# Attention scores as two matmuls of 128 rows instead of one of 128 and one of 64

## Chip, cores and metric

The kernel runs on one core of one Trainium2 chip. The metric is the device time of one execution in microseconds (us), lower is better; the median of the timed runs stands for a kernel.

## The reference

Two layers of a decoder trunk on 512 tokens of width 1024, in float32. Each layer projects the modulated and normalised tokens once (`h @ w_in`), feeds three mixers with the columns (a state-space mixer, a stick-breaking attention with 8 heads of 64, and a sparse attention with 8 query heads of 64 on 2 key heads, whose keys an indexer with 8 heads of 64 chooses), merges the three with gates, and ends in a squared-ReLU MLP. Three places multiply queries with keys over 64 channels; they are what the change touches:

```python
# stick-breaking attention, per block of 128 queries
z = jnp.einsum("bthd,bshd->bhts", q[:, s0:e0], k[:, :e0]) * scale
# sparse attention: the indexer's scores ...
logits = jnp.einsum("bthd,bsd->bths", q_idx[:, s0:e0], k_idx[:, :e0]) * (IDX_DIM ** -0.5)
# ... and the attention's own
s = jnp.einsum("btgrd,btkgd->btgrk", qb, k_sel) * scale
```

## The kernel before

All products of float32 numbers are made in parts: a number is kept as H, rounded to the matmul's fp32r format, and L, the rest. A projection (`mm3`, L198 to L201) is three matmuls into one PSUM bank: H with H, L with H and H with L. `tile_trunk` makes the whole program. Projections are jobs of 256 columns, cut into pieces of four blocks of 128 rows of the contraction; a piece's weights are loaded on SP's queue (`emit_split`, L448), rounded on ACT (L460) and their rest is taken on DVE (L461), two pieces ahead. Between the projections run streams of other work, one generator each: `scores` (the indexer), `topk`, `sbatt`, `dsa`, `ssd`. `run` (L504) is a planner: it adds up estimated costs of PE and DVE and emits the next step of a stream or the next two blocks of a projection. The order of emission is the priority of the scheduler that orders each engine's instructions; the list `ORDER` (L39) gives the order of the jobs.

The score product is `qk` (L212 to L216). A block of two heads comes out of a projection with the upper head on partitions 0 to 63 and the lower one on 64 to 127. `stack` (L203) makes of it one tile for each head, over all 128 partitions, with three copies on SP's queue (L209): for queries the head's H part above its L part, for keys its H part twice. Then one matmul over 128 rows (L215) gives (H + L of q) with H of k, and a second over the head's own 64 rows (L216) gives H of q with L of k, which is read from the tile that the evacuation left. Query tiles are the stationary operand (128 columns), keys the moving one (128 to 512 columns, by the causal block).

`qk` is called 24 times a layer by `scores` (L798; its key is doubled by ACT copies at L693 and L694), 32 times by `sbatt` (L858) and 32 times by `dsa` (L976). Keys come from the four jobs `qk0` to `qk3` (`evac_hl`, L823) and from `dkv` (`evac_dkv`, L957). All these tiles come from the pool `pa` of 26 tiles of 128 x 512 (L159). `fin` of `sbatt` (L901) ends a block of two heads and gives back its tiles; it is `sb.0` to `sb.3` in the planner's names. The projections have three accumulator banks, `acc` (L177), and a job takes two; the scores have two banks, `qk` (L180).

Of the kernel before, what the change touches and what calls it, by code (L numbers as in the profile page):

```python
# [17 lines left out]
P = 128  # L18
# [39 lines left out]
class Piece:  # L58
    """A part of a job's weights along the contraction."""

# [9 lines left out]
class Unit:  # L70
    """The products of a piece with some of the tokens."""

# [11 lines left out]
class Job:  # L84
    """A projection of one or two blocks of 128 columns, cut along its contraction."""

# [20 lines left out]
def paired(fin, a, b):  # L107
    """The units of two jobs, both with the first half of the tokens before the second."""
    a.fin = b.fin = fin
    a.left = b.left = 2  # L110
    ps = a.pieces() + b.pieces()
    for p in ps:
        p.keep = True
    return [Unit(p, c) for c in HALVES for p in ps]


class Stream:
    """Work beside the projections. A step yields its cost in us on PE and DVE and is told when its results are
    expected; it can also yield the time before which the next step is not to be emitted, or what it needs finished."""

# [30 lines left out]
def tile_trunk(ctx: ExitStack, tc: tile.TileContext, io, out, depth=DEPTH):  # L151
# [50 lines left out]

    def stack(H, L, same):  # L203
        """For the upper and the lower head of a block, one tile each over all partitions: the parts of the head,
        or its first part twice; the first part stays on the partitions that it was on."""
        B = pa.tile([P, T], F32R, name="paS", tag="pa")
        S = H if same else L
        for o, i in ((B[64:128, :], H[64:128, :]), (B[0:64, :], S[64:128, :]), (H[64:128, :], S[0:64, :])):
            sync.dma_start(o.bitcast(F32), i.bitcast(F32))  # L209
        return H, B, L  # L210

    def qk(ps, q, k, hh, cq, ck):  # L212
        """Three products of parts of 64 rows, two of them in one pass"""
        r = slice(hh * 64, hh * 64 + 64)
        pe.matmul(ps, q[hh][:, cq], k[hh][:, ck], start=True, stop=False)  # L215
        pe.matmul(ps, q[hh][r, cq], k[2][r, ck], start=False, stop=True)  # L216

    # ---- vectors of the layers, as columns over the partitions
    rows = [pa.tile([P, P], F32, name="rows", tag="pa") for _ in range(3)]
# [3 lines left out]
    sync.dma_start(crow, io["c"].rearrange("o (r c) -> (o r) c", c=P))  # L223
    # ---- constants
    slab = const.tile([P, 3216], F32, name="slab")
# [20 lines left out]

    # ---- silu(c) as columns
    cth = fixed(NK)
# [8 lines left out]
    tc.keep_in_program_order(act.preload_act_table_set("natural_log_exp_and_others"))  # L257
    # a column that adds up what the first of 32 partitions hold, for each half of the partitions
    pick = fixed(2)
# [38 lines left out]
    def ada_first(i):  # L298
        """What two of the blocks of 128 channels of layer 0 need first, shift and scale: two parts of 256 columns, each
        in two halves along the contraction, on PE beside each other in its columns."""  # L300
        wv = io["ada_w"][0].rearrange("(k p) c -> p k c", p=P)
# [49 lines left out]
    def rstd_cols(s_, r_, q_):  # L351
        """From sums of squares, one token on a partition"""
        dve.tensor_scalar(s_, s_, 1.0 / D, EPS, op0=ALU.mult, op1=ALU.add)
        act.activation(r_, s_, AF.Ln)
        act.activation(r_, r_, AF.Exp, scale=-0.5)
        dve.tensor_mul(q_, r_, r_)
        dve.tensor_mul(q_, q_, s_)
        dve.tensor_scalar(q_, q_, -0.5, 1.5, op0=ALU.mult, op1=ALU.add)
        dve.tensor_mul(r_, r_, q_)

    # ---- x, feature-major, and the norm of its tokens
    xin = [None] * 4
# [17 lines left out]

    # ---- norms
    class SumSq:
# [4 lines left out]
        def tile(self, key, c):  # L387
            """A temporary, the same one for both halves of the tokens"""
            if c == ALL:
                return tmp()  # L390
            if key not in self.kept:
                self.kept[key] = tmp()
            return self.kept.pop(key) if c == HALVES[1] else self.kept[key]
# [27 lines left out]
    class Modulated:  # L421
        """x normalised, scaled and shifted per channel, in two parts"""

# [74 lines left out]
    def later(f, lat=1.8):  # L498
        """Have f emitted when what has been emitted so far is expected to be done."""
        j = clock["job"]  # L500
        j.open += 1
        waiting.append((max(clock["pe"], clock["dve"]) + lat, j, f))

    def run(items, ahead=2, step=2):  # L504
        """Emit the units of the jobs in order and the steps of the streams between them. The order of emission
        is the scheduler's priority, so a step is emitted when its operands are expected to be there."""
        live = []
# [112 lines left out]
    def begin(l):  # L620
        """What the layer needs from its start on."""
        ly = {"A1": fixed(8), "A2": fixed(8),
              "h": Modulated(), "rs": rstd_tile()}
        return ly
# [8 lines left out]
    def layer(l, lys):  # L633
# [12 lines left out]

        # ---- small vectors of the SSD mixer
        dtb = fixed(1)[:16, :]
# [25 lines left out]

        # ---- index key, index weights, dt
        iwT = fixed(24).rearrange("p (a b) -> p a b", a=3)
# [9 lines left out]
        def evac_misc(i, ps):  # L686
# [7 lines left out]
            act.copy(iL[64:128, :], iL[0:64, :])  # L694
            st["ik"] = (iH, iH, iL)

# [7 lines left out]
        def dtprep():  # L704
            # D per channel
            dsr = fixed(8)[:16, :]
# [8 lines left out]
            dve.tensor_scalar(na, na, -1.0, None, op0=ALU.mult)  # L715
            # dt = softplus(raw + bias)
            s8 = st["dt"]
# [13 lines left out]
            yield 0, 3.4, 3.0  # L731
            # dt * a and its running sum in each chunk
            dve.tensor_scalar(u, g, na, None, op0=ALU.mult)
# [16 lines left out]
            yield 0.4, 0.4  # L750
            # the sum of each chunk on all partitions
            dg = fixed(64)[:16, :].rearrange("p (a b) -> p a b", a=16)
# [16 lines left out]
        def evac_iq(j):  # L769
            def f(i, ps):  # L770
                H, L = hl()
                rope(ps, H, L)
                iq[2 * j + i] = stack(H, L, False)
            return f

        # ---- the indexer: scores and the top 128 of each row
        sc = [None] + [tf.tile([P, T], F32, name="sc", tag="acb", bufs=6)[:, :(tb + 1) * P] for tb in range(1, 4)]
# [40 lines left out]

        # ---- stick-breaking attention
        sbt = {}  # L820
        ysb = yp.tile([P, 4, T], F32R, name="ysbH", tag="yH"), yp.tile([P, 4, T], F32R, name="ysbL", tag="yL")

        def evac_hl(key):  # L823
            def f(i, ps):
                H, L = hl()
                split(ps, H, L)
                sbt[key[i]] = stack(H, L, i == 1)
            return f
# [15 lines left out]
        def sbatt():  # L844
            """Per head: weights = sigmoid(z) times the product of (1 - sigmoid(z)) over the later keys."""
            qunits = [[3], [2, 0], [1]]
# [45 lines left out]
            def d_step(j, po, two):  # L892
                """both heads of a block beside each other in the columns of PE"""
                vb = sbt["v", j].rearrange("p (t d) -> p t d", t=4)
# [50 lines left out]

        # ---- sparse attention
        ydsa = [None, None]
        dq = {}

        def evac_dq(j):  # L950
            def f(i, ps):
                H, L = hl()
                rope(ps, H, L, 0.125)
                dq[2 * j + i] = stack(H, L, False)
            return f

        def evac_dkv(i, ps):  # L957
            if i == 0:
                H, L = hl()
                rope(ps, H, L)  # L960
                dq["k"] = stack(H, L, True)
            else:
                evac_v([None, "dv"])(1, ps)

        def dsa():
# [31 lines left out]
            def d_step(tb, g, po, a, s):  # L997
                """the upper and the lower heads of the blocks beside each other in the columns of PE"""
                av = a.rearrange("p (a b t) -> p b a t", a=2, b=2)
# [52 lines left out]

        # ---- SSD mixer
        sd = {}
# [55 lines left out]
        def ssd():  # L1110
            sst["ss"] = SumSq()

            def tok(qd, cp, sc_):
                """x token-major times a factor per token and head, for two chunks, in two parts"""
                xs = [sd["xs", 2 * qd], sd["xs", 2 * qd + 1]]
# [16 lines left out]
            def prep(qd, q):  # L1132
                """chunk states and what they give: y = D x + the part from earlier chunks"""
                g = qd // 2
# [48 lines left out]
            def e_step(qd, n):  # L1183
                """decay between the tokens of a chunk times C B"""
                h = 4 * qd + n
# [14 lines left out]
            def d_step(q, m, two):  # L1200
                """two heads beside each other in the columns of PE"""
                pd = qk_bank()
# [54 lines left out]

        # ---- merge
        mg = {}
# [175 lines left out]

        # ---- MLP
        w_up = io["w_up"][l].rearrange("(k p) c -> p k c", p=P)
# [88 lines left out]

    # ---- the start: what the first half of the contraction needs, then the second
    lys = {}
# [74 lines left out]
```

## Time and profile before

| | us |
|---|---|
| timed runs | 2067.71, 2056.53, 2066.98 |
| median | 2066.98 |
| profiled execution: span from the first to the last instruction | 2054.7 |
| PE busy | 2029.1 (99%), 9940 matmuls |
| DVE busy | 1282.9 (62%) |
| ACT busy | 879.6 (43%) |
| mean granted TensorE clock | 0.987 |

The profile is one execution; it lists its span, and not what the timed run has around it. PE is the engine of the matmuls, PEld its weight loads, DVE the vector engine, ACT the scalar engine, SP the engine whose queue issues most transfers. A matmul's duration runs from its start to the end of its last result, so consecutive ones overlap; how long a stream takes is read from their starts. Shapes are given as rows x columns of the stationary operand and then the output.

### The profile page before, as it was taken

Reading aid. Unit: us, or ns where it says so; the run is one execution under the profiler, and the core shown is the slowest. Engines: PE = TensorE matmul, PEld = TensorE weight load, DVE = VectorE, ACT = ScalarE, POOL = GpSimd, SP = SyncE. Lnnn points to the kernel's source line nnn. Section 1 sums busy time; section 2 is a strip of 40 time slices with the busy share of each in tenths; the row PEclk is TensorE's granted clock in tenths of the full one; section 3 lists DMA queues with packets and bytes.
Section 4 is the critical chain, followed back from the end, with each engine's and each line's share of the span. In section 5 each row is a group of like instructions: output and inputs, shape, how many; then the busy total and the mean of one; then the engine's idle time right before and its main releaser. Section 6 shows DMA issues by size and latency. Waiting matters only on the chain.

```text
span 2054.7 us, 26669 instructions
## 1 busy us (share of the span) xinstructions
PE 2029.1 (99%) x9940; PEld 1622.4 (79%) x9940; DVE 1282.9 (62%) x2368; ACT 879.6 (43%) x1562; POOL 86.1 (4%) x135
## 2 busy tenths in 40 slices
PE   8999999999999999999999999999999999999998
PEld 5667777588888988888896777767888898888887
DVE  4779767887846887333476985578576473333334
ACT  4444543743434533242444535267235254233343
POOL 0100110000000000000000101101000000000000
PEclk9879999999999999999999999999999999999999
DMA  9724254354344686332334423414333332323221
GB/s 293 221 83 138 69 140 122 108 163 133 115 133 144 225 294 233 93 103 92 112 98 115 113 77 75 113 52 129 108 103 108 123 113 83 99 94 105 93 93 42
DMA packets 247222, 254.36 MB, mean 124 GB/s; under 512 B 33348, under 2 KB 207732, under 8 KB 247092
## 3 DMA queue, kind: packets, MB, share of 16 engines
q1 hardware_dynamic: 246512, 252.52, 40.2%
q8 instruction: 78, 1.28, 0.2%
q14 instruction: 52, 0.43, 0.1%
q10 hardware_dynamic: 356, 0.14, 0.0%
q0 software_dynamic: 224, 0.00, 0.0%
HBM read 232.81 MB, written 6.42 MB: 116 GB/s over the span
## 4 chain that ended last, share of the span: by engine, by line
PE 95%; DMA 2%; DVE 1%; ACT 0%; issue 0%; POOL 0%; SPq 0%; ACTq 0%; POOLq 0%; DVEq 0%
PE acc L199 26%; PE acc L200 26%; PE acc L201 26%; PE qk L216 3%; PE qk L215 2%; PE tr L992 1%; PE po L1001 1%; PE tr L885 1%; PE po L898 1%; PE qk L1207 1%; PE po L201 1%; PE po L200 1%; PE po L199 1%; DMA araw<-in_ada_w_dram 1%; PE qk L199 1%; PE qk L200 1%
## 5 line engine op out<-in xcount | busy, mean ns | idle before, releaser
L199 PE MATMUL acc<-aH,wH 128*128 128x512 f32 x1544 | 619.0, 401 | 1.0 <-DVE tmp L665 0.6
L201 PE MATMUL acc<-aH,wL 128*128 128x512 f32 x1544 | 610.3, 396 | 0.9 <-DVE wL L461 0.9
L200 PE MATMUL acc<-aL,wH 128*128 128x512 f32 x1544 | 609.7, 395 | 0.0
L460 ACT CAST wH<-raw 128x1024 fp32r<-128x1024 f32 (+2 forms) x290 | 295.2, 1026 | 306.4 <-PE acc L200 269.0
L461 DVE TENSOR_TENSOR wL<-raw,wH 128x1024 fp32r<-128x1024 f32 (+2 forms) x290 | 342.9, 1198 | 24.5 <-PE acc L201 11.4
L199 PEld LDWEIGHTS acc<-aH,wH 128*128 128x128 f32 x1544 | 292.0, 189 | 69.8 <-issue 10.5
L201 PEld LDWEIGHTS acc<-aH,wL 128*128 128x128 f32 x1544 | 291.9, 189 | 64.8 <-issue 2.4
L200 PEld LDWEIGHTS acc<-aL,wH 128*128 128x128 f32 x1544 | 292.3, 189 | 60.7 <-issue 3.8
L199 PE MATMUL acc<-uH,wH 128*128 128x512 f32 x448 | 174.9, 390 | 0.0
L201 PE MATMUL acc<-uH,wL 128*128 128x512 f32 x448 | 174.6, 390 | 0.0
L200 PE MATMUL acc<-uL,wH 128*128 128x512 f32 x448 | 174.3, 389 | 0.0
L193 DVE TENSOR_TENSOR uL<-tmp,uH 128x512 fp32r<-128x512 f32 x64 | 43.9, 691 | 188.4 <-ACT uH L192 188.3
L1494 ACT ACTIVATE tmp<-acc 128x512 f32<-128x512 f32 x60 | 35.3, 593 | 220.0 <-PE acc L201 220.0
L1507 DVE SCALAR_TENSOR_TENSOR x<-acc,slab,x 128x512 f32<-128x512 f32 (+1 forms) x64 | 43.8, 716 | 129.2 <-PE acc L201 129.2
L334 DVE SCALAR_TENSOR_TENSOR aacc<-araw,slab,aacc 128x512 f32<-128x512 f32 x140 | 104.6, 753 | 7.0 <-DMA araw<-in_ada_w_dram 5.4
L201 PEld LDWEIGHTS acc<-uH,wL 128*128 128x128 f32 x448 | 84.1, 188 | 17.4
L200 PEld LDWEIGHTS acc<-uL,wH 128*128 128x128 f32 x448 | 84.1, 188 | 17.4
L199 PEld LDWEIGHTS acc<-uH,wH 128*128 128x128 f32 x448 | 84.1, 188 | 17.2
L873 DVE TENSOR_TENSOR_SCAN tmp<-tmp 128x512 f32<-128x512 f32 (+1 forms) x64 | 52.5, 824 | 31.2 <-ACT tmp L866 31.1
L666 POOL TENSOR_TENSOR tmp<-tmp,slab 128x512 f32<-128x512 f32 (+1 forms) x20 | 31.6, 1578 | 720.2 <-DVE tmp L665 689.9
L1315 DVE SCALAR_TENSOR_TENSOR tmp<-tg,acc 128x512 f32<-128x512 f32 x16 | 11.0, 685 | 68.2 <-PE acc L201 68.2
L813 DVE MAX8 m<-sc 128x8 f32<-128x256 f32 (+2 forms) x96 | 52.8, 554 | 1.0
(307 smaller groups left out, 3071.5 us busy)
## 6 DMA issues: line engine op xcount, KB each, us to landing
araw<-in_ada_w_dram SPq DMA_DIRECT2D x192, 256.0 KB, 5.3
raw<-in_w_in_dram SPq DMA_DIRECT2D x96, 512.0 KB, 3.8
raw<-in_w_up_dram SPq DMA_DIRECT2D x64, 512.0 KB, 4.6
raw<-in_w_down_dram SPq DMA_DIRECT2D x64, 512.0 KB, 3.7
raw<-in_w_in_dram SPq DMA_DIRECT2D x56, 256.0 KB, 4.4
acb<-acd SPq DMA_DIRECT2D x32, 256.0 KB, 4.5
raw<-in_w_br_ssd_dram SPq DMA_DIRECT2D x16, 512.0 KB, 5.1
raw<-in_w_out_dram SPq DMA_DIRECT2D x16, 512.0 KB, 4.2
```

Source lines behind the costliest of these rows:

```text
L193: dve.tensor_sub(L, src, H)
L199: pe.matmul(ps, a[0], b[0], start=start, stop=False)
L200: pe.matmul(ps, a[0], b[1], start=False, stop=False)
L201: pe.matmul(ps, a[1], b[0], start=False, stop=stop)
L215: pe.matmul(ps, q[hh][:, cq], k[hh][:, ck], start=True, stop=False)
L216: pe.matmul(ps, q[hh][r, cq], k[2][r, ck], start=False, stop=True)
L334: dve.scalar_tensor_tensor(a, raw, cs[:, k:k + 1], a, op0=ALU.mult, op1=ALU.add)
L460: act.copy(H[:, :w], src)
L461: dve.tensor_sub(L[:, :w], src, H[:, :w])
L813: dve.max(out=m8, in_=sc[tb])
L873: dve.tensor_tensor_scan(out=nv, data0=nv, data1=nv, initial=1.0, op0=ALU.mult, op1=ALU.bypass)
L1507: dve.scalar_tensor_tensor(xt[m][:, c], ps[:, c], mod[l][:, M_G2 + m:M_G2 + m + 1], xt[m][:, c], op0=ALU.mult, op1=ALU.add)
```

## The change

`qk` becomes two matmuls of 128 rows with the same stationary tile: the head's H above L with the key's H part twice, and again with the key's L part twice. `stack` keeps its form for queries only, and a new helper, `twice`, makes two pairs of tiles of a key block: its H part twice for each head, and its L part twice for each head. It adds a tile and three copies for a key block. The product of L with L, which was left out before, is now included. The index key already had both parts on both halves, and its tuple is written anew.

```diff
-    def stack(H, L, same):
+    def stack(H, L):
         B = pa.tile([P, T], F32R, name="paS", tag="pa")
-        S = H if same else L
-        for o, i in ((B[64:128, :], H[64:128, :]), (B[0:64, :], S[64:128, :]), (H[64:128, :], S[0:64, :])):
+        for o, i in ((B[64:128, :], H[64:128, :]), (B[0:64, :], L[64:128, :]), (H[64:128, :], L[0:64, :])):
             sync.dma_start(o.bitcast(F32), i.bitcast(F32))
-        return H, B, L
+        return H, B
+
+    def twice(H, L):
+        out_ = []
+        for X in (H, L):
+            B = pa.tile([P, T], F32R, name="paS", tag="pa")
+            for o, i in ((B[64:128, :], X[64:128, :]), (B[0:64, :], X[64:128, :]), (X[64:128, :], X[0:64, :])):
+                sync.dma_start(o.bitcast(F32), i.bitcast(F32))
+            out_.append((X, B))
+        return out_
 
     def qk(ps, q, k, hh, cq, ck):
-        r = slice(hh * 64, hh * 64 + 64)
-        pe.matmul(ps, q[hh][:, cq], k[hh][:, ck], start=True, stop=False)
-        pe.matmul(ps, q[hh][r, cq], k[2][r, ck], start=False, stop=True)
+        for n in range(2):
+            pe.matmul(ps, q[hh][:, cq], k[n][hh][:, ck], start=n == 0, stop=n == 1)
...
-            st["ik"] = (iH, iH, iL)
+            st["ik"] = ((iH, iH), (iL, iL))
...
-                iq[2 * j + i] = stack(H, L, False)
+                iq[2 * j + i] = stack(H, L)
...
-                sbt[key[i]] = stack(H, L, i == 1)
+                sbt[key[i]] = (stack, twice)[i](H, L)
...
-                dq[2 * j + i] = stack(H, L, False)
+                dq[2 * j + i] = stack(H, L)
...
-                dq["k"] = stack(H, L, True)
+                dq["k"] = twice(H, L)
```

## Rows read from the trace of the kernel before

**Rows 1.** The page's chain that ended last, by engine and by line.

```profile
PE 95%; DMA 2%; DVE 1%; ACT 0%; issue 0%; POOL 0%; SPq 0%; ACTq 0%; POOLq 0%; DVEq 0%
PE acc L199 26%; PE acc L200 26%; PE acc L201 26%; PE qk L216 3%; PE qk L215 2%; PE tr L992 1%; PE po L1001 1%; PE tr L885 1%; PE po L898 1%; PE qk L1207 1%; PE po L201 1%; PE po L200 1%; PE po L199 1%; DMA araw<-in_ada_w_dram 1%; PE qk L199 1%; PE qk L200 1%
```

**Rows 2.** The matmuls of L216: durations in ns, first and last start, shapes.

```profile
L216 PE MATMUL qk<-paL,paH x88: 322/435/792, 75.0 to 1387.9; 64*128 64x256 f32 x24, 64*128 64x384 f32 x24, 64*128 64x512 f32 x24, 64*128 64x128 f32 x16
L216 PE MATMUL qk<-paL,paS x88: 322/435/792, 76.3 to 1393.6; 64*128 64x256 f32 x24, 64*128 64x384 f32 x24, 64*128 64x512 f32 x24, 64*128 64x128 f32 x16
```

**Rows 3.** Timeline of PE, one pair of 512 columns: start us, duration us, what.

```profile
142.31 0.39 PE L201 MATMUL acc<-aH,wL 128*128 128x512 f32 x1
142.53 0.39 PE L215 MATMUL qk<-paS 128*128 128x512 f32 x1
142.85 0.49 PE L216 MATMUL qk<-paL,paS 64*128 64x512 f32 x1
143.27 0.50 PE L199 MATMUL acc<-aH,wH 128*128 128x512 f32 x1
143.61 0.40 PE L200 MATMUL acc<-aL,wH 128*128 128x512 f32 x1
```

**Rows 4.** Timeline of the weight loads of the same pair; idle before in brackets.

```profile
142.31 0.19 PEld L215 LDWEIGHTS qk<-paS 128*128 128x128 f32 x1
142.85 0.18 PEld L216 LDWEIGHTS qk<-paL,paS 64*128 64x128 f32 x1 [0.35 <-issue]
```

**Rows 5.** Timeline of PE, a pair of 256 columns, second layer.

```profile
1092.72 0.28 PE L215 MATMUL qk<-paH 128*128 128x256 f32 x1
...
1093.57 0.40 PE L200 MATMUL acc<-aL,wH 128*128 128x512 f32 x1
```

**Rows 6.** Timeline of PE, projections of 256 columns in a row.

```profile
674.49 0.28 PE L199 MATMUL qk<-aH,paH 128*128 128x256 f32 x1
674.61 0.28 PE L200 MATMUL qk<-aL,paH 128*128 128x256 f32 x1
```

**Rows 7.** L216 alone in one stretch: stretch, us, PE and PEld busy, PEclk, DMA.

```profile
88.40:125.90 37.50, 12.98 (x18) 5.13 (x18) 0.50 0.34 94
```

**Rows 8.** Timeline of PE inside that stretch.

```profile
114.48 0.63 PE L200 MATMUL acc<-aL,wH 128*128 128x512 f32 x1
114.91 0.63 PE L215 MATMUL qk<-paH 128*128 128x512 f32 x1
...
117.64 0.79 PE L201 MATMUL acc<-aH,wL 128*128 128x512 f32 x1
```

**Rows 9.** Six stretches: us, PE, PEld, DVE, ACT, POOL busy, PEclk, DMA share, GB/s.

```profile
73.00:124.00 51.00, 49.43 (x122) 27.83 (x122) 31.64 (x67) 21.13 (x39) 0.88 (x3) 0.65 0.48 130
137.00:300.00 163.00, 163.00 (x748) 121.78 (x747) 136.35 (x285) 79.09 (x137) 22.08 (x38) 1.00 0.44 123
324.00:420.00 96.00, 95.21 (x459) 64.79 (x458) 71.14 (x192) 57.97 (x138) 3.69 (x6) 0.98 0.34 103
1092.00:1124.00 32.00, 32.00 (x117) 19.18 (x117) 25.61 (x55) 16.70 (x33) 3.26 (x4) 1.00 0.40 109
1124.00:1290.00 166.00, 166.00 (x758) 123.17 (x759) 128.86 (x286) 83.39 (x146) 19.01 (x40) 1.00 0.32 87
1320.00:1400.00 80.00, 78.86 (x364) 52.68 (x363) 51.84 (x155) 45.90 (x112) 3.28 (x5) 0.96 0.26 77
```

**Rows 10.** The copies of L209 on SP's queue: ns, first and last; landing us.

```profile
L209 SPq DMA_DIRECT2D paS<-paH x44: 461/467/587, 57.8 to 1315.5; - x44
...
DMA to landing us min/median/max: 2.2/2.3/4.4
```

**Rows 11.** Timeline of ACT: ends of `sb.0` and `sb.1` (L901), `qk2`'s evacuation (L192).

```profile
180.64 0.60 ACT L901 ACTIVATE ysbH<-po 128x512 fp32r<-128x512 f32 x1 [3.01 <-PE po L898]
...
189.16 0.59 ACT L192 CAST paH<-acc 128x512 fp32r<-128x512 f32 x1 [3.93 <-PE acc L201]
...
234.11 0.58 ACT L901 ACTIVATE ysbH<-po 128x512 fp32r<-128x512 f32 x1
```

## The prediction, made before the changed kernel was run

> **What bounds the kernel now.** I read the chain of waits first. It gives TensorE (PE) 95% of the span, and the two lines of the score product (L215 and L216) 5% of it, so about 103 us of 2054.7 [rows 1]. The reader should see that nothing else holds the end for long: a microsecond taken from PE is a microsecond of the kernel unless another engine becomes late. The second view is the list of one line's instructions, for the counts: L216 runs 88 times on the one key tile and 88 times on the other, so there are 176 score products, 48 each of 512, 384 and 256 columns and 32 of 128 [rows 2]. The third is the timeline of PE around one product, read by starts and not by durations, since the passes overlap. In the stream of projections a 512-column pass starts 0.22 to 0.23 us after the one before it. The 64-row pass starts 0.32 us after the 128-row one, the next projection 0.42 us after that, and the one behind it 0.34 us later [rows 3]. The weight loads say why: the load of the 128-row pass begins while the pass before it streams, but that of the 64-row pass begins only with its own pass, after 0.35 us of idle [rows 4]. So changing from 128 rows to 64 and back is paid at both edges.
>
> **The change, part by part.**
>
> *The second pass grows to 128 rows.* With 512 columns, from the start of L215 to the second start behind the pair is 143.61 - 142.53 = 1.08 us [rows 3]. Three equal 128-row passes would take 3 x 0.227 = 0.68, so the pair costs 0.40 us too much. With 256 columns the same stretch is 1093.57 - 1092.72 = 0.85 us [rows 5]; two passes of 256 columns at the stream's 0.12 us and a projection at 0.227 make 0.47 [rows 3, 6], so 0.38 too much. The excess hardly depends on the width: it is an edge, not a streaming time. The operation that replaces it, two 128-row passes into one bank with the same stationary tile, is not in the trace. The nearest rows are the three passes of a projection, which also accumulate in one bank, and I take their step. Bounds: 0 saved, if the second load of the same tile can't go ahead; 0.40 saved by the stream. I take 0.38, nearest to the stream, and 176 x 0.38 = 67 us.
>
> *The low clock.* In the score stage of the first layer the granted clock is 0.50 (1.2 GHz) for 37.5 us, with 18 of the pairs in it [rows 7]. There two pairs of 512 columns take 117.64 - 114.91 = 2.73 us, where four projection steps of 0.43 would take 1.72 [rows 8]: 0.50 too much per pair, so 18 x (0.50 - 0.38) = 2 us more. Ahead of the fall PE ran score pairs between small transposes; it rose behind the pairs, in unbroken projections. The same stage of the second layer keeps 1.00 [rows 9]. If the change leaves no broken stretch, the clock could stay up or recover at once: about 30 projection passes at 0.23 instead of 0.43 give 6 us, 36 score passes at half of their low-clock time, (8 x 0.86 + 8 x 0.64 + 2 x 0.43) / 2 by their widths, another 6. Bounds 0 and 12 us. I take 6, since the rows show a stage at either level and the pairs are only one of the things in it.
>
> PE alone: 67 + 2 + 6 = 75 us.
>
> *What is late next.* The six stages that hold the pairs show VectorE (DVE) close behind PE [rows 9]. Second layer's scores: DVE is busy 25.6 of 32.0 us, so of 24 x 0.38 = 9 us at most 6.4 can come off unless its work moves; I take 6. First layer's scores: 6 x 0.38 + 18 x 0.50 + 6 = 17 us would leave 51 - 17 = 34 against DVE's 31.6; I take 13. The two stick-breaking and two sparse stages hold 32 pairs each, 12 us each: 163 - 12 = 151 against 136.4, 166 - 12 = 154 against 128.9, 96 - 12 = 84 against 71.1, 80 - 12 = 68 against 51.8. DVE fits, at 76% to 90%, but with chains through ScalarE (ACT) and back; I take 80% of 4 x 12 = 39 us. Sum: 13 + 6 + 39 = 58 us.
>
> *The lower key part held twice.* Each of ten key blocks (four `qk` jobs and `dkv`, two layers) gets one more tile and three more copies of 128 KB on SP's queue. A copy issues in 0.47 us and lands after 2.3 us [rows 10]. The third copy overwrites what the second reads, so it can hold the queue until that has landed: 3 x 0.47 + 2.3 = 3.7 us for a block, and behind it wait the weight loads of the projections and the `ada` loads. I cost this at nothing, because weights are issued two pieces ahead and a piece of four rows of blocks keeps PE for 24 x 0.227 = 5.4 us; if that cover is gone, it costs up to 10 x 3.7 = 37 us. The other end is 0: nothing of it can gain. No first use is near: `qk2`'s evacuation starts at 189.2 us and its heads come after the end of `sb.1` at 234.1 [rows 11]. The index key was already held twice in both parts, so it adds nothing.
>
> *Queries and labels.* Only the tuple shrinks: the lower query tile was read by nothing but its copies. No cost, no gain.
>
> The sum is against the profiled execution: 2054.7 us of span, to 1996.7. What lies around the span isn't in the page; the timed runs are 1.8 to 13.0 us above it, their median 12.3, which I keep: 1996.7 + 12.3 = 2009 us.
>
> **The rivals.**
>
> *A: the edges go and most of it reaches the end.* 2009 us; from 2067 - 82 = 1985 (all of PE's 75 us, and 6 more from the clock) to 2030. For: [rows 1, 3, 4]. Chance 0.70.
>
> *B: DVE becomes the bound.* PE's edges go, but the stages stop at DVE's and ACT's pace: 8 us in the first scores, 3 in the second, half of 48 in the others, 35 us together: 2032 us, up to 2045. For: DVE's 78% to 84% in three stages [rows 9]. Against: it is idle there while PE is not, so it waits for PE. Chance 0.15.
>
> *C: the second load can't go ahead.* Every 128-row pass of the pair would then start like the one behind the change of rows, 0.34 us after the last [rows 3], and so would the projection behind it: 3 x 0.34 = 1.02 against 1.08 us, 0.06 x 176 = 11 us, 2056 us. The Trainium skill (TensorE: Matmul & The Clock Gate, Part 3, The mechanism) speaks for this: it says that a weight load overlaps a running matmul only when its row group differs, and both passes now use all rows. The trace disagrees: loads over all 128 rows go ahead in every step of the stream, and it is the load with other rows that waits [rows 4]. Chance 0.03.
>
> *D: the copies eat the gain.* SP's 37 us come onto the path and DVE takes what B says: 35 - 37, about 2069 us, no change. For: L209's copies sit in the same queue as the weights. Against: the cover of 5.4 us per piece. Chance 0.06.
>
> *E: slower, by the pool of 26 tiles.* A `qk` block now holds six tiles instead of five. If `qk2` is evacuated before the heads of `qk0` are done, the pool would hold 3 x 6 for `qk0`, `qk1` and `qk3`, 2 for `v0`, and 3 + 4 for `qk2`, so 27 of 26, where now it is 15 + 2 + 6 = 23. The evacuation would wait for `sb.0`, holding two of the three accumulator banks, and projections stop. Now `sb.0` ends 8.5 us before [rows 11]. The price of a wait is at most the distance between the ends of two such steps, 234.1 - 180.6 = 53 us, in each layer: 2 x 53 - 58 = 48 us slower, 2115 us. It decides from (58 + 10) / 2 = 34 us per layer. Chance 0.06.
>
> **How the numbers follow.** The likeliest is A, 2009 us. A and B hold 0.85; the range goes from A's end, 1985, to B's, 2045, and leaves out C, D, E and what little lies below. About 0.5% (10 us) is what a measurement of this kernel can tell from no change. Faster: A, B and C, 0.88 (C by a hair). Same: D, 0.06. Slower: E, 0.06.
>
> **What would show it.** Right: in the timeline both score passes start 0.22 us after one another at 512 columns, the load of the second has no idle ahead of it, and the projection behind starts at the stream's step; the two score lines fall from 5% of the chain to about 3%; the first score stage spends less than 37 us at 0.50, and the six stages shorten by some 14, 6 and four times 10 us. B would show as waits of PE's loads for DVE in these stages, C as an idle ahead of the second load, D as ACT's weight casts waiting for w_in, E as ACT's evacuation of `qk2` behind the end of `sb.0` with PE idle. The prediction is wrong if the schedule of the whole program comes out in another order, since a planner places every step and I assume that it leaves them where they are.

## The result, and the profile after

| | before | after |
|---|---|---|
| median of 4 runs, us | 2061.76 | 1994.89 |
| lowest and highest, us | 2056.06, 2067.71 | 1993.62, 1997.39 |
| profiled execution: span, us | 2054.7 | 1992.6 |
| PE busy, us | 2029.1 | 1955.4 |
| mean granted clock | 0.987 | 0.996 |

The ratio of after to before is 0.969, with a 95% interval of 0.966 to 0.972: 3.1% faster. The forecast was 2009 us, with a range of 1985 to 2045 and 0.88 for faster. The time is 14 us under the forecast.

The chain of waits of after, from its page (shares of the span, by engine and then by line; L225 is the line of the score matmuls now):

```profile
PE 88%; DVE 7%; DMA 2%; issue 1%; ACT 1%; POOL 0%; SPq 0%; ACTq 0%; POOLq 0%; DVEq 0%
PE acc L199 25%; PE acc L201 25%; PE acc L200 25%; PE qk L225 2%; DVE wL L470 1%; PE po L1010 1%; PE tr L1001 1%; DVE sc L823 1%; DVE m L822 1%; DVE tmp L882 1%; PE po L907 1%; PE qk L1216 1%; PE tr L894 1%; DMA araw<-in_ada_w_dram 1%; PE po L201 1%
```

Against [rows 1], the score lines fall from 3% and 2% to 2% together, and DVE goes from 1% to 7%, with the top-k lines L822 and L823 in it, which the chain of before did not show. So the edges left PE's path, and DVE took a part of it.

The edges themselves are seen in PE's timeline of after, around a pair of 512 columns (start us, duration us, what), and in the timeline of the weight loads of two such pairs in a row:

```profile
106.70 0.39 PE L201 MATMUL acc<-aH,wL 128*128 128x512 f32 x1
106.93 0.39 PE L225 MATMUL qk<-paH 128*128 128x512 f32 x1
107.15 0.39 PE L225 MATMUL qk<-paL,paH 128*128 128x512 f32 x1
107.38 0.39 PE L199 MATMUL acc<-aH,wH 128*128 128x512 f32 x1
107.61 0.39 PE L200 MATMUL acc<-aL,wH 128*128 128x512 f32 x1
```

```profile
100.05 0.19 PEld L225 LDWEIGHTS qk<-paH 128*128 128x128 f32 x1
100.28 0.19 PEld L225 LDWEIGHTS qk<-paL,paH 128*128 128x128 f32 x1
100.51 0.19 PEld L225 LDWEIGHTS qk<-paH,paS 128*128 128x128 f32 x1
100.74 0.19 PEld L225 LDWEIGHTS qk<-paL,paS 128*128 128x128 f32 x1
100.97 0.19 PEld L201 LDWEIGHTS acc<-aH,wL 128*128 128x128 f32 x1
```

From the first pass of the pair to the second start behind it is 107.61 - 106.93 = 0.68 us, where before had 1.08 [rows 3]. Each pass starts 0.22 to 0.23 us after the one before it, and no load has idle ahead of it, where the 64-row load had 0.35 us [rows 4]. With 256 columns the second pass starts 0.11 us after the first.

What took part of the gain back is in PE's waits of after, the two longest that before did not have (engine and line, what it waited for: us in total, times, longest), and in PE's timeline:

```profile
PE acc L199 <- DVE paL L193: 5.0, 1, 5.0
PE acc L199 <- DVE ysbL L911: 3.4, 1, 3.4
```

```profile
161.82 0.76 PE L225 MATMUL qk<-paS 128*128 128x384 f32 x4
162.42 0.62 PE L894 MATMUL tr<-slab,tmp 128*128 128x128 f32 x4
168.02 0.80 PE L199 MATMUL acc<-aH,wH 128*128 128x512 f32 x1 [4.98 <-DVE paL L193]
168.61 0.63 PE L200 MATMUL acc<-aL,wH 128*128 128x512 f32 x1
169.04 0.63 PE L201 MATMUL acc<-aH,wL 128*128 128x512 f32 x1
```

The next job's projection needs an accumulator bank, and the bank comes free when DVE has taken the rest of a key block out of it (L193). DVE's timeline shows what stands ahead of that instruction:

```profile
163.14 0.55 DVE L823 MATCH_REPLACE8 sc<-m,sc 128x384 f32<-128x384 f32 x1
163.60 0.14 DVE L885 TENSOR_SCALAR tmp<-tmp 128x1 f32<-128x1 f32 x1
163.72 0.56 DVE L822 MAX8 m<-sc 128x8 f32<-128x384 f32 x1
...
166.22 1.15 DVE L822 MAX8 m<-sc 128x8 f32<-128x384 f32 x2
167.29 0.67 DVE L193 TENSOR_TENSOR paL<-acc,paH 128x512 fp32r<-128x512 f32 x1
```

From 163.07 to 167.29 DVE runs top-k almost back to back while PE has nothing. PE then comes back at the lower clock: projection passes step by 0.43 us from 168.61 to 172.45. The wait in the second layer, at 1133.85, looks the same: L911 starts at 1133.12 behind top-k, and from 1135.42 to 1138.41 the passes step by 0.43 us.

Last, the stretches of [rows 9] in after. The first is the same stretch; the second and third hold the work of [rows 9]'s two stick-breaking stages, 25 to 27 and 45 to 50 us earlier (columns as there):

```profile
73.00:124.00 51.00, 49.23 (x235) 39.50 (x233) 48.43 (x110) 33.22 (x61) 4.73 (x8) 1.00 0.78 208
112.10:272.60 160.50, 155.42 (x748) 122.46 (x747) 138.70 (x290) 77.59 (x138) 22.43 (x38) 0.98 0.51 136
1079.30:1239.80 160.50, 156.84 (x760) 123.32 (x759) 132.15 (x290) 82.46 (x147) 19.87 (x40) 0.99 0.39 100
```

The first stretch went from clock 0.65 to 1.00 and holds 235 matmuls instead of 122. In the other two PE, which was busy all the time before, is idle for 5.1 and 3.7 us.

Where the time went is read by counting the projections' matmuls (L199 to L201) and comparing the start of the same one in both traces:

```
work of before, us                      gain of after by its end   in the stage   predicted
first scores (73 to 137)                24.9                       24.9           13
first stick-breaking (to 300)           27.4                        2.5           10
first sparse (to 420)                   38.7                       11.3           10
up to the second scores (to 1092)       38.2                       -0.5            0
second scores (to 1124)                 44.8                        6.6            6
second stick-breaking (to 1290)         50.4                        5.6           10
second sparse (to 1400)                 63.0                       12.6           10
to the end                              62.9                       -0.1            0
```

### The profile page after: what moved, and what is told of

The parts are those of the page before. It is cut to its first block, busy times and chain, and to the rows that moved or that the text cites. A ratio compares the mean times of both kernels' runs of the same rounds, so it can differ in the third digit from the quotient of the medians.

```text
span 1992.6 us, 26735 instructions
## 1 busy us (share of the span) xinstructions
PE 1955.4 (98%) x9940; PEld 1609.0 (81%) x9940; DVE 1279.8 (64%) x2368; ACT 872.1 (44%) x1562; POOL 87.9 (4%) x135
## 4 chain that ended last, share of the span: by engine, by line
PE 88%; DVE 7%; DMA 2%; issue 1%; ACT 1%; POOL 0%; SPq 0%; ACTq 0%; POOLq 0%; DVEq 0%
PE acc L199 25%; PE acc L201 25%; PE acc L200 25%; PE qk L225 2%; DVE wL L470 1%; PE po L1010 1%; PE tr L1001 1%; DVE sc L823 1%; DVE m L822 1%; DVE tmp L882 1%; PE po L907 1%; PE qk L1216 1%; PE tr L894 1%; DMA araw<-in_ada_w_dram 1%; PE po L201 1%
## 5 line engine op out<-in xcount | busy, mean ns | idle before, releaser
L199 PE MATMUL acc<-aH,wH 128*128 128x512 f32 x1544 | 612.3, 397 | 9.4 <-DVE paL L193 5.0
L201 PE MATMUL acc<-aH,wL 128*128 128x512 f32 x1544 | 606.7, 393 | 0.9 <-DVE wL L470 0.8
L200 PE MATMUL acc<-aL,wH 128*128 128x512 f32 x1544 | 605.7, 392 | 0.0
L470 DVE TENSOR_TENSOR wL<-raw,wH 128x1024 fp32r<-128x1024 f32 (+2 forms) x290 | 343.0, 1198 | 18.8 <-ACT wH L469 7.9
L199 PEld LDWEIGHTS acc<-aH,wH 128*128 128x128 f32 x1544 | 290.8, 188 | 72.0 <-DVE paL L193 5.7
L201 PEld LDWEIGHTS acc<-aH,wL 128*128 128x128 f32 x1544 | 290.8, 188 | 62.6 <-DVE wL L470 2.2
L200 PEld LDWEIGHTS acc<-aL,wH 128*128 128x128 f32 x1544 | 291.2, 189 | 57.7 <-issue 0.7
L199 PE MATMUL acc<-uH,wH 128*128 128x512 f32 x448 | 174.9, 390 | 0.0
L201 PE MATMUL acc<-uH,wL 128*128 128x512 f32 x448 | 174.6, 390 | 0.0
L200 PE MATMUL acc<-uL,wH 128*128 128x512 f32 x448 | 174.3, 389 | 0.0
L193 DVE TENSOR_TENSOR uL<-tmp,uH 128x512 fp32r<-128x512 f32 x64 | 43.9, 692 | 187.8 <-ACT uH L192 187.8
L201 PEld LDWEIGHTS acc<-uH,wL 128*128 128x128 f32 x448 | 84.1, 188 | 17.6
L200 PEld LDWEIGHTS acc<-uL,wH 128*128 128x128 f32 x448 | 84.1, 188 | 17.3
L199 PEld LDWEIGHTS acc<-uH,wH 128*128 128x128 f32 x448 | 84.1, 188 | 17.1
L822 DVE MAX8 m<-sc 128x8 f32<-128x256 f32 (+2 forms) x96 | 52.6, 551 | 1.2 <-POOL sc L800 0.2
```

Of the source, the lines that this page charges most:

```text
L193: dve.tensor_sub(L, src, H)
L199: pe.matmul(ps, a[0], b[0], start=start, stop=False)
L200: pe.matmul(ps, a[0], b[1], start=False, stop=False)
L201: pe.matmul(ps, a[1], b[0], start=False, stop=stop)
L470: dve.tensor_sub(L[:, :w], src, H[:, :w])
L822: dve.max(out=m8, in_=sc[tb])
```

## The experiments

All ratios are to the kernel before on the same chip, with 95% intervals. The tables of gains go by the same count of projections.

**Do the copies and the new order matter without the 128-row passes?** The changed kernel with the second pass back on 64 rows:

```diff
-        for n in range(2):
-            pe.matmul(ps, q[hh][:, cq], k[n][hh][:, ck], start=n == 0, stop=n == 1)
+        r = slice(hh * 64, hh * 64 + 64)
+        pe.matmul(ps, q[hh][:, cq], k[0][hh][:, ck], start=True, stop=False)
+        pe.matmul(ps, q[hh][r, cq], k[1][hh][r, ck], start=False, stop=True)
```

> The changed kernel with its second score pass back on 64 rows; the doubled lower key part and its copies stay. Theory of the edges (the gain is the change of rows and the clock that came with it): the time is that of the kernel before, 2062 us within 10, and the first score stage runs at 0.50 again. Rival (the gain came from another order of the program, or from tiles and copies): it stays below 2030 us. Copies not hidden: above 2070 us.

2044.49 us, ratio 0.994 [0.992, 0.997]. That is neither of the two values: with the same passes as before and 30 copies more, the kernel is no slower and a little faster. The whole difference is gained in the first score stage (15.7 us between 75 and 137 us of the profiled executions, and 1.5 us either way at most afterwards), and the stage's line says why:

```profile
73.00:124.00 51.00, 49.43 (x189) 32.00 (x188) 40.87 (x87) 28.97 (x52) 2.62 (x6) 1.00 0.64 169
```

The clock is 1.00, where the same 64-row pairs had 0.65 in [rows 9]. What differs on PE is only the order: the copies moved some of the scheduler's choices, and in the traces 106 of PE's 9940 matmuls stand in other places than in before, all of them between 84 and 136 us. So the fall of the clock does not follow from the pairs alone. This is one profiled execution: six of the ten runs lie at 2041 to 2045 us like it, with a mean clock of 0.995 to 0.998, and four at 2050 to 2053 us with 0.990 to 0.992; where those four lost their time is not known. From here to after, the 128-row passes give 49.6 us, 0.28 for each of 176 pairs; in the first score stage, at 1.00 in both, 24.8 - 15.7 = 9.1 us, 0.38 for each of 24.

**Do the copies cost anything?** The changed kernel without the copies of the lower key part; the second pass multiplies 128 rows of the unstacked tile, which holds the L parts of both heads. The query's H still meets its own head's L, but the query's L meets the L of the other head, a small product that does not belong there:

```diff
-        for X in (H, L):
-            ...
-            out_.append((X, B))
-        return out_
+        B = pa.tile([P, T], F32R, name="paS", tag="pa")
+        for o, i in ((B[64:128, :], H[64:128, :]), (B[0:64, :], H[64:128, :]), (H[64:128, :], H[0:64, :])):
+            sync.dma_start(o.bitcast(F32), i.bitcast(F32))
+        return [(H, B), (L, L)]
```

> The changed kernel without the copies of the lower key part (the second pass of 128 rows reads the part as it was left, so the scores of the key blocks are not the right ones): the price of the tile and the three copies. Copies hidden: 1995 us within 6. Copies on the path: up to 37 us less, 1958 us, and least of all places in which a wait ahead of the score passes names a DMA.

1987.47 us, ratio 0.966 [0.963, 0.968]; 7.4 us under after. In the traces DVE keeps the order of before in all its 2368 places, where after has 286 changed, and the two waits of 5.0 and 3.4 us are gone. The first stretch is at 1.00 here too, with before's order on PE (one score pass stands three places later) and without 64-row passes:

```profile
73.00:124.00 51.00, 49.32 (x238) 40.26 (x237) 49.26 (x115) 33.58 (x63) 4.36 (x8) 1.00 0.75 208
```

**Is it the transfers or the order that they force?** The same copies on POOL's queue instead of SP's, and beside it the changed kernel once more:

```diff
-                sync.dma_start(o.bitcast(F32), i.bitcast(F32))
+                (sync if X is H else pool).dma_start(o.bitcast(F32), i.bitcast(F32))
```

> The changed kernel with the copies of the lower key part issued on GpSimd's queue instead of SP's; PE's and DVE's programs then run in the order of the kernel before almost everywhere (3 of 9496 and 63 of 2254 places differ), as they did without the copies. If the 7 us that the copies cost are the other order that they force on DVE, with its waits of 5.0 and 3.4 us: 1987 us within 3, neither wait there. If they are the transfers themselves (traffic, landing times): 1995 us within 3.

> The changed kernel once more, beside the one with the copies on GpSimd's queue on the same chip: 1995 us within 3 by every theory, with the two waits of 5.0 and 3.4 us again, since they follow from the order of the program.

1990.26 us, ratio 0.968 [0.966, 0.969], against 1995.32 us, 0.970 [0.969, 0.972]: 5.1 us less, with all copies made. The changed kernel shows both waits again; with the copies on POOL's queue both are gone, though 149 of DVE's places still differ from before's, and the two stick-breaking stages gain 5.9 and 7.6 us. So most of the price of the copies is the order that they force on SP's and DVE's queues; which of the two queues matters more was not separated. What is left against the kernel without copies, 2.8 us, is small enough for the two ratios' intervals to overlap, and whether it is the transfers or order is open; one wait of PE is new here, 2.5 us for ACT's L870 that ends at 152.31 us, and from 151.9 us the clock is low for 3.4 us. This version computes all that after does, and is faster than after.

**What makes the clock fall?** That version with the second pass back on 64 rows, so before's order with before's passes and the copies out of the way:

```diff
-        for n in range(2):
-            pe.matmul(ps, q[hh][:, cq], k[n][hh][:, ck], start=n == 0, stop=n == 1)
+        r = slice(hh * 64, hh * 64 + 64)
+        pe.matmul(ps, q[hh][:, cq], k[0][hh][:, ck], start=True, stop=False)
+        pe.matmul(ps, q[hh][r, cq], k[1][hh][r, ck], start=False, stop=True)
```

> The same with the second score pass back on 64 rows: the kernel before with the copies added on GpSimd's queue, PE in its order but for one place. If the low clock of the first score stage needs that order and the 64-row passes both: the stage runs at 0.50 again and the time is that of the kernel before, 2058 us within 6. If the copies kept the clock up in the run that had them on SP's queue: 2044 us within 5.

2060.12 us, ratio 1.001 [0.998, 1.005], no change. In the traces PE's order is that of before in all 9940 places, and from 75 to 324 us every counted start lies 1.0 to 1.3 us behind before's, a difference from the start of the program. The low clock is back in full:

```profile
73.00:124.00 51.00, 49.43 (x124) 28.15 (x123) 32.31 (x68) 20.96 (x39) 2.28 (x5) 0.66 0.51 138
```

Of the four combinations, only 64-row passes in before's order fall in the profiled executions: the other three keep 1.00 (the lines above and after's). Two things follow. The long low stretch of [rows 7] came where both were there, and either part of the change alone kept the clock up. But the two together do not make it fall every time: of the 41 runs of before beside these experiments two took 2043.5 and 2043.8 us with a mean clock of 0.996, where most took 2054 to 2061 us with 0.984 to 0.989; 37.5 us at half clock are 0.009 of the mean, so the stage seems to have kept the clock in those two. And 30 copies by another queue cost nothing there, since the first layer keeps before's pace up to 324 us. In this profiled execution the clock fell in the second layer's score stage too (0.76 from 1092 to 1140 us), which costs 9 us more. The runs of this kernel reach from 2044.13 to 2069.23 us, about 16 us below and 9 us above its median. The slowest is the profiled one, in which both stages fell; that neither fell in the fastest is likely by its size but not shown.

**Do the edges add up?** The first layer's 24 score pairs alone back on 64 rows, and 128 rows in the two score stages alone:

```diff
-        for n in range(2):
-            pe.matmul(ps, q[hh][:, cq], k[n][hh][:, ck], start=n == 0, stop=n == 1)
+        r = slice(hh * 64, hh * 64 + 64)
+        s = slice(0, P) if full_ else r
+        pe.matmul(ps, q[hh][:, cq], k[0][hh][:, ck], start=True, stop=False)
+        pe.matmul(ps, q[hh][s, cq], k[1][hh][s, ck], start=False, stop=True)
...
# scores passes full_ = (l > 0) in the one, True in the other; the other calls pass True and False
```

> The changed kernel with the second score pass back on 64 rows only in the indexer's scores of the first layer (24 of the 176 pairs). If the low clock of that stage came from the 64-row pairs: the stage runs at 0.50 again for tens of us and the time is some 9 + 15 = 24 us above the changed kernel, about 2018 us. If it did not: 24 x 0.38 = 9 us above, about 2004 us, and the stage stays at 1.00, as it did with 64-row pairs and the copies.

> 128 rows only in the indexer's scores (48 of the 176 pairs), 64 rows in the second pass of the other 128; all copies as in the changed kernel. If the first score stage keeps the full clock: 19 us in the first layer and 9 in the second, about 2034 us. If the clock falls there as before, 18 us in all, about 2044 us. Sum of parts: the other 128 pairs are then worth what is left to 1995 us, some 40 to 50 us.

The first took 2005.57 us, ratio 0.974 [0.971, 0.977]: 24 pairs cost 10.5 us against the mean of after's two medians (1995.1), 0.44 each. The projection counts put it in that stage: 9.5 us between 75 and 137 us, and no more later. The stage's clock is 0.97, some 3.4 us at the lower level, of which 3.4 / 2 = 1.7 us are lost, so (9.5 - 1.7) / 24 = 0.33 us are a pair's edges. The second took 2029.99 us, 0.986 [0.983, 0.989]: 14.5 us under the kernel with 64 rows everywhere, 0.30 for each of its 48 pairs, and the remaining 128 pairs give the other 35 us, 0.27 each. So the pairs add up, at 0.27 to 0.38 us.

**Is it the narrow pass or the change of rows?** Both passes on the head's own 64 rows, which leaves the query's lower part out of the computation:

```diff
+        r = slice(hh * 64, hh * 64 + 64)
         for n in range(2):
-            pe.matmul(ps, q[hh][:, cq], k[n][hh][:, ck], start=n == 0, stop=n == 1)
+            pe.matmul(ps, q[hh][r, cq], k[n][hh][r, ck], start=n == 0, stop=n == 1)
```

> The changed kernel with both score passes on the 64 rows of the head (the product of the lower query part is left out). Edges cost, not narrow passes: where a pair follows a pair nothing changes rows any more, which is so for some 46 of the 176 pairs in the trace before; these get 0.38 us cheaper each, so about 2062 - 17 = 2045 us, and inside a pair the second pass starts 0.22 to 0.23 us after the first at 512 columns. Rival, a 64-row pass is slow in itself: 0.42 us a pass, 352 passes, so 2062 us or more.

2030.59 us, ratio 0.987 [0.984, 0.989]; 14 us under the kernel with one pass of 64 rows, so the rival's 2062 us or more is out. I had set 17 us for the pairs that follow one another and so lose edges, but counted them from a base at the low clock, so the time missed by 14 us. The step inside a pair, expected at 0.22 to 0.23 us, was missed too. PE's timeline of a single pair, twice 64 rows between projections:

```profile
137.35 0.39 PE L201 MATMUL acc<-aH,wL 128*128 128x512 f32 x1
137.66 0.49 PE L226 MATMUL qk<-paH 64*128 64x512 f32 x1
138.00 0.39 PE L226 MATMUL qk<-paL,paH 64*128 64x512 f32 x1
138.32 0.50 PE L199 MATMUL acc<-aH,wH 128*128 128x512 f32 x1
138.66 0.40 PE L200 MATMUL acc<-aL,wH 128*128 128x512 f32 x1
```

From L201 to L200 it takes 1.31 us, where four steps of the stream take 0.91: 0.40 too much, as in before. All four steps are long, 0.31 to 0.34 us, so an edge falls on the pass at the change of rows and on the one behind it, and two narrow passes pay the same two edges as one. That a 64-row pass is not slow in itself shows where more than two follow each other:

```profile
149.87 0.44 PE L226 MATMUL qk<-paH 64*128 64x384 f32 x1
150.14 0.33 PE L226 MATMUL qk<-paL,paH 64*128 64x384 f32 x1
150.31 0.22 PE L226 MATMUL qk<-paH 64*128 64x128 f32 x1
```

The first step is an edge's, 0.27 us; the second is 0.17, and the median step of score passes of 384 columns over 128 rows in after is 0.175 us. So fewer channels make no pass shorter, and a run of narrow passes is no slower than one of wide passes. In the score stages above all, the passes of the two heads of a block, one on rows 0 to 63 and one on rows 64 to 127, can even run beside each other:

```profile
88.46 0.45 PE L226 MATMUL qk<-paH,paS 64*128 64x384 f32 x1
88.46 0.44 PE L226 MATMUL qk<-paH 64*128 64x384 f32 x1
88.74 0.33 PE L226 MATMUL qk<-paL,paS 64*128 64x384 f32 x1
88.75 0.34 PE L226 MATMUL qk<-paL,paH 64*128 64x384 f32 x1
89.01 0.50 PE L199 MATMUL acc<-aH,wH 128*128 128x512 f32 x1
```

Two pairs take 0.55 us up to the projection behind them, where four steps of 0.175 make 0.70. Only 23 of the 352 passes start so, within 0.02 us of another; a kernel that puts its heads side by side on purpose was not tried.

**Is DVE's amount of work the new bound?** Half of the top-k rounds, so that 64 keys are chosen instead of 128, in after and in before:

```diff
-                for r in range(16):
+                for r in range(8):
```

> The changed kernel with 8 rounds of the top-k instead of 16 (it chooses 64 keys instead of 128, so the masks are not the right ones): some 24 us a layer less work on DVE in the stretch after the scores. If DVE has become the bound there: PE's waits go and the stretch gets shorter by about what the pairs were worth and did not bring, 20 us for both layers, about 1975 us. If PE still bounds: 1995 us within 5.

> The kernel before with 8 rounds of the top-k instead of 16 (64 keys instead of 128), beside the same cut in the changed kernel. If DVE became the bound by the change only, the cut is worth little here: within 6 us of the kernel before, as far as the clock of the first score stage lets one see. If DVE bounded that stretch already before: 15 us or more less.

In after 1993.0 us, 0.968 [0.965, 0.970]; in before 2061.83 us, 1.002 [0.999, 1.004]. DVE has less to do in the stretch of the 5 us wait (columns as above; after, then with half of top-k):

```profile
130.00:180.00 50.00, 44.92 (x204) 35.00 (x203) 49.83 (x117) 18.76 (x31) 3.96 (x8) 0.93 0.58 153
```

```profile
130.00:180.00 50.00, 46.73 (x227) 36.77 (x226) 42.35 (x86) 24.53 (x42) 7.68 (x11) 1.00 0.67 191
```

but the time does not follow: the two stick-breaking stages gain 6.0 and 3.4 us, together 9.4, where after has 2.5 and 5.6, together 8.1. Waits of the same kind stand elsewhere:

```profile
PE acc L199 <- DVE paL L193: 3.5, 1, 3.5
PE tr L894 <- DVE tmp L885: 3.3, 2, 2.4
```

So the theory that DVE's throughput bounds these stages falls. What the traces show is the order of its queue: an evacuation that releases PE stands behind work that nobody waits for yet, and the kernel without the copies, with the full top-k, has neither long wait.

**Does a bank that ACT frees help?** In the key blocks' evacuation (L835) ACT copies the bank out first, and DVE works from the copy:

```diff
-                split(ps, H, L)
+                w = tmp()
+                act.copy(w, ps)
+                act.copy(H, w)
+                dve.tensor_sub(L, w, H)
```

> The changed kernel, but the evacuation of the stick-breaking queries and keys first copies the bank into a tile on ACT, and the parts are made from the tile, so that a projection's bank no longer waits for DVE's subtraction behind the top-k. If the two new waits of PE (5.0 and 3.4 us, with 10 us of low clock behind them) are the price of that order: both go, 8 to 13 us less than the changed kernel, about 1984 us. Rival, DVE is the bound of that stretch whoever frees the bank: the waits move to the next operation that DVE owes PE, and the time stays at 1995 us within 4.

1991.89 us (1991.70 to 1992.32), ratio 0.967 [0.964, 0.970]: 3 us under after, at the edge of the rival's range and short of the 8 to 13 us. The stages say more for the first theory than the time: in the profiled execution the two stick-breaking stages gain 6.5 and 7.0 us (after 2.5 and 5.6), while 3.4 us were lost before 73 us, where the edit changes nothing. The 5.0 us wait is gone, but PE now waits 2.4 us for ACT's copy, 2.4 for DVE's `ysbL`, and 3.5 in five places for DVE's `wL`. The wait for L911 in the second layer was not tried by itself; what of that instruction PE needs is open.

## Why the prediction was right, point by point

The span came within about 4 us of its forecast in part by luck: the first scores gave 12 us more than was set for them and the two stick-breaking stages 12 us less. The mechanism of the edges was right; the sizes of these stages were not.

**The edges.** Right in kind and size: both passes and the projection behind them keep the stream's step, as the timelines of after show, and the first score stage, compared with 64-row passes in the same order and at the same clock, gives the forecast 0.38 us a pair. The two sparse stages give 11.3 and 12.6 us, where 12.2 was PE's own share, but not all of it is edges: before ran 3.4 and 6.8 us of them at a clock of 0.50 (the 0.98 and 0.96 of [rows 9]) and after none, which is 1.7 and 3.4 us. That leaves 9.6 and 9.2 us, close to the 10 that were set, and the clock of these stages is a term that the prediction did not have.

**The low clock.** Right in direction, too small: 2 + 6 us taken, 2 + 12 at the upper end. The kernel with after's order and 64-row passes gains 15.7 us in that stage without any wider pass, so the step that was mis-sized is the choice of the middle between two bounds where the stage went all the way to 1.00. By the whole stretch, 37.5 us at half the full clock, up to 37.5 / 2 = 18.8 us could be won. With it the first scores gave 24.9 us instead of 13. The cap of 13 from DVE's 31.6 us of work failed too: a projection that began at 125.1 us of before begins at 98.0 in after, 25 us into the stage, too early for 31.6 us of DVE's work to be done, so some of that work fell behind the projections.

**What is late next.** The four stages with DVE close behind were taken at 80% of 12 us. The sparse ones kept about that share, the stick-breaking ones 2.5 and 5.6 us. In the first, 5.1 us are PE's idle, and 10 projection steps of 0.43 instead of 0.23 are 2 us: 2.5 + 5.1 + 2 = 9.6 of 12.2. In the second, 5.6 + 3.7 + 8 x 0.2 = 10.9. That is rival B's mechanism in small: PE waits for DVE in these stages, by the order of DVE's queue and not by its load, as the half top-k shows. Without the two long waits, as with the copies on POOL's queue, these stages give 5.9 and 7.6 us, still under 10; where the rest is was not settled. The second scores gave 6.6 us, as forecast (6).

**The copies.** Put at nothing, with 37 us as the other end. Measured: 7.4 us, of which 5.1 go with another queue. The step that failed is that only waiting on SP's queue was weighed; the price came through the scheduler, which placed DVE's instructions otherwise. The prediction had named this as what would make it wrong ("comes out in another order").

**Around the span.** Taken as 12.3 us, the median of the runs above the profiled span. The runs show 1.7 and 1.8 (1994.34 us for a span of 1992.6, 2056.53 for 2054.7). The rest was no overhead but the spread of before's runs. With 1.8 the forecast would have been 1998.5; this term alone is 10 of the 14 us that it missed by. The span was forecast at 1996.7 and came at 1992.6.

**The rivals.** C is excluded by the loads at 100.28 and 100.74 us, which go ahead of their passes at 100.51 and 100.97 while a pass over the same 128 rows runs. The Trainium skill (TensorE: Matmul & The Clock Gate, Part 3, The mechanism) says that a load overlaps a running matmul only when its row group differs, though elsewhere in the section it excepts a load into the background weight buffer. By the first alone this trace contradicts it; which buffer a load goes to no row here shows. The runs here put going to 64 rows and back at 0.27 to 0.40 us. The Trainium skill (TensorEngine Tiling (Array Packing), Key Properties) says that changing the tiling mode drains TensorE, which fits such edges; it gives no price. D is excluded by the kernel with copies and 64-row passes, no slower than before. E's price, some 50 us a layer, shows nowhere. One wait of PE, the 3.4 us in the second layer, does end at an instruction of `fin` (L911), but that stood behind top-k on DVE, and the prediction's chain through the evacuation of `qk2` is not seen.

## What to carry to other kernels

Read a change of matmul rows as an edge, paid on the way in and on the way out whatever the width of the passes, and price it by the starts of the passes behind it; filling the array with a product that is not needed can be cheaper than a single narrower pass among wide ones. Add what lies around the span from the run that was profiled, not from the spread of the other runs. Where a scheduler orders the queues, added transfers can cost by the places that they move on other engines: put them on a queue that nothing urgent shares, and look at what stands ahead of each evacuation that gives a bank back.

## What the runs showed of the hardware that was not expected

The granted clock of one stage stood at 0.50 (1.2 GHz) for 37.5 us with PE 97% busy in the stage [rows 7, 9], and at 1.00 (2.4 GHz) in the profiled executions in which the passes were widened to 128 rows or some 100 places of PE's order in the stage were others. What sets it off is not settled: ahead of the fall stand 64-row pairs among small transposes, the three combinations that lack either the pairs or that order keep 1.00, and two of before's 41 runs seem to have kept it as well. A wait can also cost more than its length: the 5.0 us and 3.4 us waits of after are each followed by a stretch of 3 to 4 us in which passes step by 0.43 us, some 2 us more. And a pass over 64 rows is not shorter than one over 128: at a change of rows passes of 512 columns step by 0.31 to 0.34 us, where the stream's step is 0.23, and in a run of 64-row passes 384 columns step by 0.17 us, as over 128 rows. What 64 rows can gain is that two passes on different halves of the rows run beside each other, with starts 0.01 us apart.
